# Retention's score-times-value products written ahead of every read of their PSUM bank, with the keys' transpose in the other bank, and the rotation tables fetched from GpSimd's queue

## The chip, the cores and the metric

The kernel runs on one core of a Trainium2 chip. The metric is the device time of one execution in microseconds (us); the time of a kernel is the median of its runs. A core has five engines with instruction streams of their own: TensorE (PE in the profile; its weight loads are shown as PEld), VectorE (DVE), ScalarE (ACT), GpSimd (POOL) and SyncE (SP), which here only issues transfers. Each engine takes its instructions in a fixed order, and an instruction whose operands aren't ready holds up what is written behind it on that engine. TensorE writes its results into PSUM, which is divided into eight banks of 512 float32 per partition; VectorE and ScalarE read them from there. Transfers between DRAM and SBUF are issued from a queue of SyncE, ScalarE or GpSimd.

## The reference

One decoder layer over 2048 positions of width 1024, causal, batch 1, in float32. A normalised and modulated input `h` goes through one projection of 9216 columns, whose parts feed two sequence mixers: HGRN2 (a gated linear recurrence, 8 heads, states of 128 x 128) and multi-scale retention (8 heads, keys of 64, values of 128). Both are normalised by head, gated, mixed and projected out. The change touches retention, which the reference computes in chunks of 128 positions:

```python
scores = einsum('bhnid,bhnjd->bhnij', qc, kc) * Dm[:, None]
intra = einsum('bhnij,bhnje->bhnie', scores, vc)
chunk_state = einsum('bhnjd,bhnde->...', kc * zeta, vc)     # summed over the chunk's positions j
R_next = chunk_decay * R + chunk_state
cross = einsum('bhnid,bhnde->bhnie', qc * xi, R)
o = intra + cross
```

`q` and `k` are rotated first, which needs tables of cosines and sines by position:

```python
rotary(t) = concatenate([t1 * cos - t2 * sin, t1 * sin + t2 * cos])
```

## The kernel before

**Projection.** The 2048 positions are worked in two halves of 1024 (`sb` 0 and 1), each in two blocks of 512. The projection's columns are cut into groups of 256, called quads; `ORDER` lists them: `a` (HGRN2's forget gate and query of a head), `v` (a value group of both mixers), `b` (retention's q and k of a pair of heads), `A` and `B` (the gates). Each quad is computed by a Strassen-like scheme of seven products instead of eight. A product has 12 matmuls of 128 x 512 (float32 split in a high and a low part, three matmuls for each of four k-tiles). TensorE's instructions are kept in program order by the class `InOrder` (L70 for matmuls, L73 for transposes), so the order in which the Python code writes them is the order of execution. For the other engines a planner orders the instructions, by priorities and by a model of costs: the splitting of weights (`Weights.split`, tiles `b` from `w`; ScalarE at L295, VectorE at L296 and L416) has 400 steps of priority, the evacuation of products (`after`, tiles `c`, `x`, `vt`) 600. Three buffers hold split weights (`NBW`), four hold temporaries (tag `tp`, `NTP`), and PSUM's eight banks are shared out as `x0`, `x1`, `v` (products), `lv` (HGRN2's tree), two of tag `o` and one tile `rt` of two banks.

**Background.** The mixers run between the products as generators, called lanes. `Background.tick` counts one for each k-tile of a product, and when eight have gone by (`GAP`) a `burst` takes each lane one step on: retention's lane first, then HGRN2's `tree` and `hgrn_out`. A lane that yields `"mid"` is taken on once more in the same burst, after the others have had their turn.

**Retention.** `retention(p, sb)` handles a pair of heads over eight chunks, in nine steps; four pairs and two halves make eight passes. In step n it begins chunk n and ends chunk m = n − 1. It has one PSUM tile of two banks, `pt` (named `rt` in the profile), and one bank of tag `o`, `po` (named `por`). The step's work is written in this order: the transpose of chunk n's keys (`kz`, in `pt`'s second bank); its scores for both heads (one in each bank of `pt`); for chunk m the part that comes from the state (`cross`, one head in `po`, the other in `pt`'s second bank); the update of the state (`x`, in `pt`'s first bank). VectorE then reads the scores and multiplies them by the decay (`scm`, L985), ScalarE reads the keys (`rkz`, L988), and VectorE reads `x` into the state `rs` (L991, or L995 in the first chunk). After `yield "mid"`, and so behind what the other lanes put on TensorE, the score-times-value products of chunk m are written: they add `scms[m]` times the values onto `pos[0]` in `po` and onto `pos[1]` in `pt`'s second bank. `normed` then takes the squares (ScalarE, L827), the reciprocal root (GpSimd, L174 or L176, and L177) and the scaled copies (ScalarE, L830) into `ur`. HGRN2's `normed` goes the same way, with `ssh`, `rrh` and `uh`. `pt` has one buffer, so step n + 1 writes it when step n has been read.

**Rotation.** `tables` writes cosines and sines (and their negative) to a DRAM tensor `lin`. For each `b` quad `load_rot` fetches, for each of two blocks, a cosine tile `ct` with one transfer (L626) and a sine tile `sn` with two (L628), broadcast over the heads, into temporaries of tag `tp`. `take_b` multiplies on VectorE (L639 to L642) and stores the rotated tiles to DRAM, from where retention reads them. The load for the first block is written ahead of the quad's first product, the one for the second block ahead of the next quad's. All transfers but the weights' are issued from SyncE's queue; the weights are issued from ScalarE's.

The functions that the change touches, and what calls them:

Of the kernel before, what the change touches and what calls it, by code (L numbers as in the profile page):

```python
# [22 lines left out]
P = 128  # L23
# [5 lines left out]
BLK = 512  # L29
# [33 lines left out]
def tile_hybrid(ctx: ExitStack, tc: tile.TileContext, a: dict, out: bass.AP):  # L63
    nc = tc.nc
    V, S, G = nc.vector, nc.scalar, nc.gpsimd
# [9 lines left out]
    PE = InOrder()  # L75
# [10 lines left out]
    def bank(name, tag):  # L86
        return pp.tile([P, 512], F32, name=name, tag=tag, bufs=small[tag])

    def tmp(name, cols=512):
        return upool.tile([P, cols], F32, name=name, tag="tp", bufs=NTP)  # L90

    def dram(name, shape):
        return dpool.tile(shape, F32, name=name, tag=name)
# [41 lines left out]
    for t in range(8):  # L135
        tag, bufs = xwhere[t]
        n = {"f": 2 * 513, "k": 1025, "q": 1024, "A": 1024}[tag]
# [465 lines left out]
    lin = dram("lin", [3, 32, L])  # L603
# [18 lines left out]
    def load_rot(q, tb):  # L622
        b = QUADS[q][0] * NBLK + tb
        ct, sn = tmp(f"ct{q}_{tb}"), tmp(f"sn{q}_{tb}")
        sl = slice(b * BLK, (b + 1) * BLK)
        nc.sync.dma_start(out=ct, in_=lin[0, :, sl].unsqueeze(0).broadcast_to([4, 32, BLK]))  # L626
        for two in range(2):
            nc.sync.dma_start(  # L628
                out=sn[64 * two : 64 * two + 64, :], in_=lin[1 + two, :, sl].unsqueeze(0).broadcast_to([2, 32, BLK])
            )  # L630
        rots[tb] = ct, sn
# [190 lines left out]
    def normed(pos, dsts, nm, eps=None):  # L822
        n = len(pos)
        ss = upool.tile([P, 2], F32, name=f"ss{nm}", tag="ss", bufs=4)
        rr = upool.tile([P, 2], F32, name=f"rr{nm}", tag="rr", bufs=4)
        for i in range(n):
            S.activation(out=junk, in_=pos[i], func=AF.Square, accum_out=ss[:, i : i + 1])  # L827
        rstd_of(rr[:, 0:n], ss[:, 0:n], P, eps)
        for i in range(n):
            S.activation(out=dsts[i], in_=pos[i], func=AF.Copy, scale=rr[:, i : i + 1])  # L830

    def send_u(s, h, b, c, u):

        def store():
            nc.sync.dma_start(out=ud[s, h, b][:, (c - 1) * P : (c + 1) * P], in_=u.rearrange("p c e -> p (c e)"))
            if c == 3:
                usent[s, h, b] = bg.now

        bg.post(5.0, store)
# [82 lines left out]
    def retention(p, sb):  # L922
        h0 = 2 * p
        g0 = sb * CH
        while rnext[0] != (sb, p):
            yield True
        rs = upool.tile([P, P], F32, name=f"rs{p}_{sb}", tag="rs", bufs=1)
        if sb:
            nc.sync.dma_start(out=rs, in_=rstd_d[p])
        qks, kzs, vrs, scms, age, u = {}, {}, {}, {}, {}, {}  # L930
        rows = [slice(64 * j, 64 * j + 64) for j in range(2)]
        dT = upool.tile([P, 256], F32, name=f"dT{p}_{sb}", tag="dT", bufs=1)
        nc.sync.dma_start(out=dT, in_=a["dT"][:, h0 * P : (h0 + 2) * P])

        def fetch(n):
            g = g0 + n
            qks[n] = upool.tile([P, 2, P], F32, name=f"rqk{p}_{g}", tag="rqk", bufs=NQP)
            sl = slice(n * P, (n + 1) * P)
            nc.sync.dma_start(out=qks[n], in_=rd[p, sb][:, :, sl].rearrange("s p t -> p s t"))
            age[n] = bg.now  # L940

        def fetch_v(n):
            g = g0 + n
            vrs[n] = upool.tile([P, 2, P], F32, name=f"vr{p}_{g}", tag="vr", bufs=2)
            sl = slice(n * P, (n + 1) * P)
            nc.sync.dma_start(out=vrs[n], in_=vdr[p, sb][:, sl, :].rearrange("j t e -> t j e"))

        n = nf = 0
        while n <= CH:
            while nf < CH and nf <= n + 1:  # L950
                b = sb * NBLK + nf // 4
                ts = [rsent.get((s, p, b)) for s in range(2)] + [vsent.get((1, h0 + j, b)) for j in range(2)]
                if any(t is None or t > bg.now - 5.0 for t in ts):
                    break
                fetch(nf)
                nf += 1
            if n < CH and (n not in age or bg.now < age[n] + 6.0):
                yield True
                continue
            if n < CH:  # L960
                fetch_v(n)
            m, g = n - 1, g0 + n - 1
            last = g == L // P - 1
            pt = pp.tile([P, 2, 512], F32, name=f"rt{p}_{g0 + n}", tag="rt", bufs=1)
            x = pt[:, 0, P : 2 * P]
            if n < CH:
                kz = pt[:, 1, 2 * P : 3 * P]
                PE.transpose(out=kz, in_=qks[n][:, 1, :], identity=ident)
                for j, r in enumerate(rows):
                    PE.matmul(out=pt[:, j, 0:P], lhsT=qks[n][r, 1, :], rhs=qks[n][r, 0, :], start=True, stop=True)  # L970
            if n:
                vb_ = [vrs[m][:, j, :] for j in range(2)]
                po = bank(f"por{p}_{g}", "o")
                pos = [po[:, 0:P], pt[:, 1, P : 2 * P]]
                if g:
                    for j, r in enumerate(rows):
                        PE.matmul(
                            out=pos[j], lhsT=qks[m][r, 0, :], rhs=rs[r, :], start=True, stop=False, skip_group_check=True
                        )
                if not last:  # L980
                    for j, r in enumerate(rows):
                        PE.matmul(out=x[r, :], lhsT=kzs[m][:, r], rhs=vb_[j], start=True, stop=True)
            if n < CH:
                scms[n] = upool.tile([P, 2, P], F32, name=f"scm{p}_{g0 + n}", tag="scm", bufs=2)
                V.tensor_tensor(out=scms[n], in0=pt[:, :, 0:P], in1=dT.rearrange("p (j t) -> p j t", j=2), op=ALU.mult)  # L985
                kzs[n] = upool.tile([P, P], F32, name=f"rkz{p}_{g0 + n}", tag="rkz", bufs=2)
                for j, r in enumerate(rows):
                    S.activation(out=kzs[n][:, r], in_=kz[:, r], func=AF.Copy, scale=zeta[:, h0 + j : h0 + j + 1])  # L988
            if n:
                if g and not last:  # L990
                    V.scalar_tensor_tensor(  # L991
                        out=rs, in0=rs, scalar=gC[:, p : p + 1], in1=x, op0=ALU.mult, op1=ALU.add
                    )
                elif g == 0:
                    V.tensor_copy(out=rs, in_=x)  # L995
                yield "mid"
                for j in range(2):
                    PE.matmul(
                        out=pos[j], lhsT=scms[m][:, j], rhs=vb_[j], start=g == 0, stop=True, skip_group_check=True
                    )  # L1000
                b = g // 4
                if m % 2 == 0:
                    for j in range(2):
                        u[j] = upool.tile([P, 2, P], F32, name=f"ur{h0 + j}_{g}", tag="ur", bufs=4)
                normed(pos, [u[j][:, m % 2, :] for j in range(2)], f"r{p}_{g}", epsx[:, h0 : h0 + 2])
                if m % 2:
                    for j in range(2):
                        send_u(1, h0 + j, b, m % 4, u[j])
                if m == CH - 1:
                    rnext[0] = (sb, p + 1) if p + 1 < NP else (sb + 1, 0)  # L1010
                    if not last:
                        nc.sync.dma_start(out=rstd_d[p], in_=rs)
            n += 1
            yield
# [297 lines left out]
    mid = max(i for i, q in enumerate(QUADS) if q[0] == 0)  # L1312
    for i in range(2, len(seq)):
        m, q = seq[i]
# [7 lines left out]
        if kind == "b" and m == 2:  # L1322
            load_rot(q, 0)
        if m == 2 and QUADS[q - 1][1] == "b":
            load_rot(q - 1, 1)
# [8 lines left out]
        if q == NQ - 1:  # L1334
# [4 lines left out]
            if m == 4:  # L1339
# [3 lines left out]
                    out=pro["fg"], in0=pro["fg"], scalar1=float(D) ** 0.5, scalar2=None, op0=ALU.mult  # L1343
# [116 lines left out]
```

## Time and profile before

| | |
|---|---|
| median of three runs | 2314.5 us (2307.4 to 2316.7) |
| the profiled execution | 2308.1 us, span 2306.3 us |
| TensorE busy | 2007.8 us, 87% |
| VectorE busy | 1426.5 us, 62% |
| ScalarE busy | 1006.0 us, 44% |
| GpSimd busy | 239.6 us, 10% |
| mean granted TensorE clock | 0.951 of full speed |
| transfers | 263 MB; SyncE's queue 27.8%, ScalarE's 11.6% of the 16 DMA engines' time |

A group row of the page names a line, an engine, an operation, the tiles it writes and reads, their shapes and the count; then the busy time, the mean of one instruction in ns, the idle time of the engine just before these instructions, and what ended most of that idle time. `rt<-vr,scm` are the score-times-value products into the tile `rt`, `b<-w` is the splitting of weights. A row of waits reads "engine, tile and line, waited for engine, tile and line: us in total, times, longest". In an answer in order of time, the brackets hold the idle time ahead of the instruction and what ended it. What ends a wait is inferred from semaphores. Idle time of an engine costs something only where the end depends on it.

### The profile page before, as it was taken

What the parts mean: (1) busy time and instruction counts of PE and PEld (TensorE: products, weight loads), DVE (VectorE), ACT (ScalarE), POOL (GpSimd) and SP (SyncE); (2) the same over time, 40 slices, a digit from 0 to 9 for tenths busy, and PEclk for the clock granted to TensorE, in tenths of its full rate; (3) what the DMA queues carried; (4) which work ended last, traced back from release to release, by engine and by line L of the source; (5) the groups of instructions that cost most, each with busy time, mean ns of one, the idle gap of its engine ahead of it and who ended that gap; (6) DMA issues with size and microseconds to landing.
All of it is one profiled execution on the core that took longest, in us unless ns stands there. A gap on an engine that the chain in (4) does not pass through costs nothing.

```text
span 2306.3 us, 39796 instructions
## 1 busy us (share of the span) xinstructions
PE 2007.8 (87%) x15108; PEld 1612.8 (70%) x15108; DVE 1426.5 (62%) x2677; ACT 1006.0 (44%) x2434; POOL 239.6 (10%) x466
## 2 busy tenths in 40 slices
PE   4878799997989698889778899997999799898998
PEld 3656588776767576668666688776777677676887
DVE  5865667565756466656765667565767575658333
ACT  5624344534455354444524444543454345444232
POOL 1001110201020110210000110101011000110000
PEclk9989999999999799989989999999999899999999
DMA  8143424242344437624434424242244424235443
GB/s 272 42 101 103 109 76 105 81 115 85 85 132 128 135 117 207 194 76 125 151 82 104 112 78 107 83 111 86 75 133 130 119 65 108 74 93 170 134 137 119
DMA packets 446016, 263.02 MB, mean 114 GB/s; under 512 B 161024, under 2 KB 395520, under 8 KB 445824
## 3 DMA queue, kind: packets, MB, share of 16 engines
q1 hardware_dynamic: 292704, 184.43, 27.8%
q10 hardware_dynamic: 153120, 76.04, 11.6%
q8 instruction: 119, 1.95, 0.4%
q14 instruction: 73, 0.60, 0.1%
HBM read 188.03 MB, written 72.35 MB: 113 GB/s over the span
## 4 chain that ended last, share of the span: by engine, by line
PE 53%; DMA 15%; DVE 14%; ACT 8%; issue 4%; POOL 4%; SPq 1%; ACTq 1%; DVEq 0%; POOLq 0%
PE x L70 22%; PE v L70 11%; PE ops L70 8%; PE y L70 5%; DVE b L296 4%; ACT b L295 2%; DVE w L416 2%; DMA w<-in_w_a_dram 2%; PE lv L70 2%; PE poh L70 2%; DMA w<-in_w_d_dram 2%; DMA rd<-c 2%; POOL rrh L177 1%; DMA sn<-lin 1%; PE rt L70 1%
## 5 line engine op out<-in xcount | busy, mean ns | idle before, releaser
L296 DVE TENSOR_TENSOR b<-w,b 128x512 fp32r<-128x512 f32 (+1 forms) x553 | 346.2, 635 | 329.0 <-ACT b L295 321.4
L295 ACT ACTIVATE b<-w 128x512 fp32r<-128x512 f32 (+1 forms) x553 | 316.7, 583 | 388.0 <-PE x L70 297.0
L70 PE MATMUL v<-S,b 128*128 128x512 f32 x1704 | 433.7, 404 | 26.5 <-ACT c L477 19.7
L70 PE MATMUL x<-S,b 128*128 128x512 f32 x1704 | 431.9, 402 | 4.8 <-DVE b L296 3.2
L70 PE MATMUL x<-A,b 128*128 128x512 f32 x1704 | 430.1, 401 | 2.3 <-ACT c L477 0.9
L70 PEld LDWEIGHTS v<-S,b 128*128 128x128 f32 x1704 | 323.7, 193 | 99.9 <-ACT c L477 22.4
L70 PEld LDWEIGHTS x<-A,b 128*128 128x128 f32 x1704 | 323.1, 193 | 70.9 <-ACT wo L295 1.3
L70 PEld LDWEIGHTS x<-S,b 128*128 128x128 f32 x1704 | 320.9, 193 | 72.5 <-DVE b L296 4.5
L70 PE MATMUL y<-A,b 128*128 128x512 f32 x840 | 221.9, 416 | 47.2 <-DVE vt L588 39.5
L416 DVE TENSOR_TENSOR w<-w,w 128x512 f32<-128x512 f32 x284 | 194.9, 687 | 66.6 <-DMA w<-in_w_a_dram 21.7
L70 PEld LDWEIGHTS y<-A,b 128*128 128x128 f32 x840 | 165.6, 201 | 84.5 <-issue 49.4
L174 POOL TENSOR_SCALAR ssh<-ssh 128x1 f32<-128x1 f32 x128 | 44.6, 349 | 1447.9 <-ACT junk L827 1447.8
L70 PE MATMUL ops<-wo,m 128*128 128x512 f32 x768 | 176.5, 392 | 0.0
L70 PEld LDWEIGHTS ops<-wo,m 128*128 128x128 f32 x768 | 145.7, 190 | 30.5
L477 ACT ACTIVATE c<-v 128x512 f32<-128x512 f32 x142 | 84.5, 595 | 119.8 <-PE v L70 109.1
L70 PE MATMUL rt<-vr,scm 128*128 128x128 f32 x128 | 32.7, 340 | 90.5 <-DVE rs L991 80.3
L830 ACT ACTIVATE uh<-poh,rrh 128x128 f32<-128x128 f32 x128 | 47.1, 368 | 142.1 <-POOL rrh L177 142.0
L497 DVE TENSOR_TENSOR c<-c,x 128x512 f32<-128x512 f32 x71 | 48.8, 687 | 88.9 <-PE x L70 88.3
L70 PEld LDWEIGHTS lv<-q,k 128*32 128x32 f32 (+1 forms) x5888 | 70.8, 110 | 45.7 <-issue 35.8
L70 PE MATMUL lv<-q,k 128*32 128x16 f32 (+2 forms) x5888 | 82.1, 188 | 19.9 <-DVE ad L788 8.2
L177 POOL TENSOR_TENSOR rrh<-ssh,mhalf 128x1 f32<-128x1 f32 x128 | 93.1, 727 | 10.6
L70 PEld LDWEIGHTS rt<-vr,scm 128*128 128x128 f32 x128 | 20.6, 202 | 101.1 <-DVE rs L991 89.7
(189 smaller groups left out, 2463.0 us busy)
## 6 DMA issues: line engine op xcount, KB each, us to landing
w<-in_w_d_dram ACTq DMA_DIRECT2D x128, 256.0 KB
w<-in_w_c_dram ACTq DMA_DIRECT2D x66, 256.0 KB
mu<-ud SPq DMA_DIRECT2D x64, 256.0 KB
w<-in_w_a_dram ACTq DMA_DIRECT2D x60, 256.0 KB
wa<-in_w_ada_dram SPq DMA_DIRECT2D x16, 512.0 KB
w<-in_w_b_dram ACTq DMA_DIRECT2D x32, 256.0 KB
vd<-vt SPq DMA_DIRECT2D x128, 64.0 KB
vh<-vd SPq DMA_DIRECT2D x64, 128.0 KB
```

The source lines that it names most:

```text
L70: return tc.keep_in_program_order(nc.tensor.matmul(**kw))
L174: G.tensor_scalar(out=ss, in0=ss, scalar1=n * EPS, scalar2=None, op0=ALU.add)
L177: G.tensor_tensor(out=dst, in0=ss, in1=mhalf.broadcast_to([P, w]), op=ALU.pow)
L295: S.activation(out=t[0], in_=src, func=AF.Copy)
L296: return V.tensor_tensor(out=t[1], in0=src, in1=t[0], op=ALU.subtract)
L416: V.tensor_tensor(out=out, in0=x, in1=y, op=ALU.add)
L477: S.activation(out=t, in_=ps, func=AF.Copy)
L497: V.tensor_tensor(out=t, in0=t, in1=xb[q], op=ALU.subtract)
L830: S.activation(out=dsts[i], in_=pos[i], func=AF.Copy, scale=rr[:, i : i + 1])
```

## The change

Two edits. In `load_rot` the three transfers of a load are issued from GpSimd's queue (`G`) instead of SyncE's. In `retention` the bank `po` is taken at the start of each step, the first one too, and holds the keys' transpose `kz` as well as `pos[0]`; the score-times-value products are written right behind the state update's matmuls, ahead of the three reads by VectorE and ScalarE; the `yield "mid"` is gone, so that `normed` too is written ahead of the other lanes' work in the burst. What is computed stays the same.

```diff
@@ load_rot
-        nc.sync.dma_start(out=ct, in_=lin[0, :, sl].unsqueeze(0).broadcast_to([4, 32, BLK]))
+        G.dma_start(out=ct, in_=lin[0, :, sl].unsqueeze(0).broadcast_to([4, 32, BLK]))
         for two in range(2):
-            nc.sync.dma_start(
+            G.dma_start(
                 out=sn[64 * two : 64 * two + 64, :], in_=lin[1 + two, :, sl].unsqueeze(0).broadcast_to([2, 32, BLK])
             )
@@ retention
             x = pt[:, 0, P : 2 * P]
+            po = bank(f"por{p}_{g0 + n}", "o")
             if n < CH:
-                kz = pt[:, 1, 2 * P : 3 * P]
+                kz = po[:, P : 2 * P]
                 PE.transpose(out=kz, in_=qks[n][:, 1, :], identity=ident)
                 for j, r in enumerate(rows):
                     PE.matmul(out=pt[:, j, 0:P], lhsT=qks[n][r, 1, :], rhs=qks[n][r, 0, :], start=True, stop=True)
             if n:
                 vb_ = [vrs[m][:, j, :] for j in range(2)]
-                po = bank(f"por{p}_{g}", "o")
                 pos = [po[:, 0:P], pt[:, 1, P : 2 * P]]
...
                 if not last:
                     for j, r in enumerate(rows):
                         PE.matmul(out=x[r, :], lhsT=kzs[m][:, r], rhs=vb_[j], start=True, stop=True)
+                for j in range(2):
+                    PE.matmul(
+                        out=pos[j], lhsT=scms[m][:, j], rhs=vb_[j], start=g == 0, stop=True, skip_group_check=True
+                    )
             if n < CH:
                 scms[n] = upool.tile([P, 2, P], F32, name=f"scm{p}_{g0 + n}", tag="scm", bufs=2)
...
                 elif g == 0:
                     V.tensor_copy(out=rs, in_=x)
-                yield "mid"
-                for j in range(2):
-                    PE.matmul(
-                        out=pos[j], lhsT=scms[m][:, j], rhs=vb_[j], start=g == 0, stop=True, skip_group_check=True
-                    )
                 b = g // 4
```

## The prediction, made before the changed kernel was run

> **What bounds the kernel now.** I read four views: the page, TensorE's waits by releaser, the eight retention passes side by side, and single steps in order of time. The page first.
>
> ```profile
> span 2306.3 us, 39796 instructions
> PE 2007.8 (87%) x15108; PEld 1612.8 (70%) x15108; DVE 1426.5 (62%) x2677; ACT 1006.0 (44%) x2434; POOL 239.6 (10%) x466
> ...
> L295 ACT ACTIVATE b<-w 128x512 fp32r<-128x512 f32 (+1 forms) x553 | 316.7, 583 | 388.0 <-PE x L70 297.0
> ...
> L70 PE MATMUL rt<-vr,scm 128*128 128x128 f32 x128 | 32.7, 340 | 90.5 <-DVE rs L991 80.3
> ```
>
> TensorE is busy 87%, and the weight splitting that feeds it (`b<-w`) spends 297.0 us waiting for TensorE to give back a buffer: on the whole TensorE sets the pace, its instructions run in written order, and a wait at its head is lost unless a later wait would have come anyway. Of its idle 298.5 us (2306.3 − 2007.8) the last row holds 90.5 in one group: retention's score-times-value products into `rt`. They number 128; the waits (total, times, longest):
>
> ```profile
> PE rt L70 <- DVE rs L991: 80.3, 48, 8.1
> ...
> PE rt L70 <- DVE rs L995: 10.1, 4, 5.6
> ...
> PE rt L70 <- ACT ur L830: 4.0, 2, 2.0
> ...
> PE x L70 <- DVE b L296: 3.2, 1, 3.2
> ```
>
> So 52 of the 64 retention steps stop TensorE for 1.74 us on average (90.5 / 52), while waits for split weights are small. One step in order of time (start, length, engine; in brackets the idle time before it and what ended it):
>
> ```profile
> 228.66 0.49 PE L70 MATMUL rt<-rqk 64*128 64x128 f32 x4
> ...
> 232.50 0.42 DVE L985 TENSOR_TENSOR scm<-rt,dT 128x256 f32<-128x256 f32 x1
> ...
> 232.96 0.52 ACT L988 ACTIVATE rkz<-rt,zeta 128x64 f32<-128x64 f32 x2 [3.18 <-DVE scm L985]
> ...
> 233.69 0.34 DVE L991 SCALAR_TENSOR_TENSOR rs<-rs,gC,rt 128x128 f32<-128x128 f32 x1
> ...
> 234.09 0.49 PE L70 MATMUL rt<-vr,scm 128*128 128x128 f32 x2 [2.33 <-DVE rs L991]
> ...
> 236.29 0.27 ACT L827 ACTIVATE junk<-rt 128x128 bf16<-128x128 f32 x1
> ...
> 237.00 0.70 POOL L177 TENSOR_TENSOR rrr<-ssr,mhalf 128x2 f32<-128x2 f32 x1
> ...
> 238.00 0.36 ACT L830 ACTIVATE ur<-rt,rrr 128x128 f32<-128x128 f32 x1
> ...
> 239.87 0.27 PE L73 MATMUL rt<-ident,rqk 128*128 128x128 f32 x1
> ```
>
> The scores stand at 229.2, but VectorE, busy with rotation and weights, reads them only at 232.50; ScalarE's key copies wait for that read, the state update for the copies, and the product, which needs none of the three results (its `scm` is the previous step's), for the state update. It is an ordering of accesses to one PSUM tile, not data.
>
> **Part 1: products ahead of the reads, keys in the other bank.** No instruction is added or removed beyond one more allocation of an "o" bank per pass (eight). Removed is the cause of the 90.5 us: all matmuls of a step, the two products included, now precede the reads of `rt`, and their operands are a step old. What follows the product on TensorE is the next projection product, 12 matmuls. How much stays won depends on what is late next.
>
> ```profile
> 193.00:290.00 97.00, 72.30 (x731) 56.49 (x730) 56.32 (x116) 39.15 (x127) 13.28 (x28) 0.93 0.38 105
> ...
> sum 683.00, PE 574.09 PEld 452.58 DVE 406.53 ACT 324.94 POOL 124.44; mean PE 71.76 PEld 56.57 DVE 50.82 ACT 40.62 POOL 15.55
> ```
>
> These are the eight retention passes (length; busy PE, weight loads, DVE, ACT, POOL; granted clock; DMA): 683 us, VectorE busy 406.5. With 90.5 us taken out VectorE would be busy 69% (406.5 / 592.5), up from 60%. It does not become the bound, but its local backlog grows, since it used TensorE's stalls to catch up. So I split the 90.5. Five waits are long:
>
> ```profile
> 210.98 0.79 PE L70 MATMUL rt<-vr,scm 128*128 128x128 f32 x2 [5.60 <-DVE rs L995]
> 270.88 0.80 PE L70 MATMUL rt<-vr,scm 128*128 128x128 f32 x2 [8.07 <-DVE rs L991]
> 943.40 0.80 PE L70 MATMUL rt<-vr,scm 128*128 128x128 f32 x2 [4.94 <-DVE rs L991]
> 1254.71 0.80 PE L70 MATMUL rt<-vr,scm 128*128 128x128 f32 x2 [5.65 <-DVE rs L991]
> 1279.93 0.79 PE L70 MATMUL rt<-vr,scm 128*128 128x128 f32 x2 [4.59 <-DVE rs L991]
> ```
>
> They sum to 28.9 us, and there VectorE itself was held or overfull; before 270.88 it stood on a weight transfer:
>
> ```profile
> 269.27 0.69 DVE L416 TENSOR_TENSOR w<-w,w 128x512 f32<-128x512 f32 x1 [5.69 <-DMA w<-in_w_a_dram]
> ...
> 271.32 4.26 PE L70 MATMUL y<-A,b 128*128 128x512 f32 x12
> 275.42 2.88 PE L70 MATMUL x<-S,b 128*128 128x512 f32 x12
> ```
>
> TensorE will run into the products already prepared (three split buffers, 2.88 us each at full rate) and then wait for the same late weights. Bounds 0 and 28.9; I take 10, two of the five as wholly won, nearer the low end because the transfer ends no sooner. The other 47 waits hold 90.5 − 28.9 = 61.6 us, 1.3 us each. Their cover is the three prepared buffers; bounds 30 (half comes back as waits for VectorE's backlog) and 61.6; I take 49, 80%, nearer the top because weight splitting is what waits for TensorE (297.0 us), not the reverse.
>
> **What the moved steps now wait for.** The key transpose writes a fresh "o" bank, and the scores write `rt`; both need the previous step's last ScalarE read, `ur`. In the step shown it ends at 238.36 and the next transpose starts at 239.87. Without the stall that start moves to 237.54; the read comes sooner too, because its squares need no matmul after the state update: that update ends at 234.03, and from square to last copy the chain above lasts 2.1 us (236.29 to 238.36 in the trace, two squares, two GpSimd instructions, two copies), so about 236.4 with the queue ahead of it. Slack stays near 1.1 us; steps with less wait. Today that wait costs 4.0 us; I let it grow by 3. On ScalarE the key copies no longer stand for VectorE; instead the squares of `rt` stand for the state update, so I count nothing there (if squares are late, the wait just named is what grows).
>
> **Part 2: tables from GpSimd's queue.** Sixteen loads, three transfers each, leave SyncE's queue for GpSimd's.
>
> ```profile
> L628 SPq DMA_DIRECT2D sn<-lin x32: 475/512/540, 120.7 to 1818.9; - x32
> ...
>   DMA sn<-lin: 32.3, 12
> ...
>   DVE sw L639: 17.4, 6
>   DVE sw L640: 14.8, 6
> ```
>
> ```profile
> L626 SPq DMA_DIRECT2D ct<-lin x16: 578/584/3318, 119.9 to 1817.5; - x16
> ```
>
> ```profile
> L174 POOL TENSOR_SCALAR ssh<-ssh x128: 218/222/1055, 185.2 to 2059.7; 128x1 f32<-128x1 f32 x128
> L177 POOL TENSOR_TENSOR rrh<-ssh,mhalf x128: 547/573/1695, 185.5 to 2060.3; 128x1 f32<-128x1 f32 x128
> ...
>   ACT uh L830: 142.0, 127
> ```
>
> SyncE spends 0.58 + 2 × 0.51 = 1.6 us issuing a load. No GpSimd issue is in this trace. Bounds: 0.51 us each (SyncE's) and 1.70 (GpSimd's longest instruction), so 1.5 to 5.1 us a load; I take 1 us each, 3 us a load, as GpSimd's ordinary instructions (0.2 to 0.6) are nearer the low end. Behind a load on GpSimd stand the norm's two instructions, on which ScalarE already waits 142.0 us. GpSimd is busy 10%, so most loads fall into gaps; at this one the next norm follows within 2.5 us:
>
> ```profile
> 1232.49 0.58 SPq L626 DMA_DIRECT2D ct<-lin  x1
> 1233.18 1.04 SPq L628 DMA_DIRECT2D sn<-lin  x2
> ...
> 1234.95 0.22 POOL L174 TENSOR_SCALAR ssh<-ssh 128x1 f32<-128x1 f32 x1 [3.89 <-ACT junk L827]
> ```
>
> I count four such meetings at 1 us, 4 us lost (bounds 0; 16 × 5.1 = 82 if every load met one). VectorE waits 32.3 us for tables already (each of the two multiplies six times: six of the eight loads for a second half block), so a later landing hits it directly, and a sooner one helps: from a queue of its own a load no longer stands behind SyncE's stores and loads. Bounds +32.3 (all gone) and −28 (eight loads × 3.5 us, 5.1 against 1.6); I take +2, the middle. SyncE's freed 26 us are worth nothing: no wait for its queue is among TensorE's.
>
> [...]
>
> **Sum.** 49 + 10 − 3 − 4 + 2 = 54 us. The profiled execution took 2308.1 us beside its span of 2306.3; 2308.1 − 54 = 2254. That execution lies near the lowest of the three runs (2307.4, 2314.5, 2316.7), about 4 us under their middle, so I say 2258 for a median. Its own range, with the 61.6 kept between 50% and 100% and the long waits between 0 and 20: 2230 to 2290.
>
> **Rivals.**
> 1. *The stall moves on.* Without its pauses VectorE falls behind and TensorE waits for split weights and evacuations instead; only a third of 61.6 is kept, none of the long ones: 20 us, about 2293. For it: VectorE's backlog caused every one of these waits. Against: the splitting waits for TensorE, and 69% is no bound.
> 2. *Slower: GpSimd's queue as the bottleneck.* A load's issue waits on GpSimd for its free temporary, as it does on SyncE now, and whatever is behind it waits too:
>
> ```profile
> 1270.30 0.58 SPq L626 DMA_DIRECT2D ct<-lin  x1
> ...
> 1275.49 1.07 SPq L628 DMA_DIRECT2D sn<-lin  x2
> ```
>
> Here 4.6 us pass between cosine and sine. With 3.5 us of slower issue and 4.6 of such waiting each load lands d = 8.1 us later, VectorE stands eight times that, 65 us, and four norms are held 4 us each, 16: 2312 − 56 + 81 = 2337. It decides from d = 5, where 40 + 16 cancel the 56 of part 1. For it: GpSimd's order is as fixed as TensorE's. Against: GpSimd idles 90%, and in the passes it is busy 124.4 of 683. [...]
> 3. *More than forecast.* All 61.6 and most of the long waits stay won, and tables land sooner and free half of the 32.3: 61.6 + 20 + 16 = 98, about 2215.
> 4. *Nothing moves.* The tile's accesses stay serialized elsewhere (the scores then wait for `ur`): about 2312.
>
> **Chances.** Forecast 0.54; stall moves on 0.17; slower 0.12; more 0.10; nothing 0.07. Three runs of this kernel scatter by 0.4%, so under 0.5% (12 us) counts as no change. Faster: 0.54 + 0.15 + 0.10 = 0.79; within: 0.02 of rival 1 and 0.07, 0.09; slower 0.12. The range 2208 to 2318 leaves out the slower case and the far end of "more".
>
> **What would show it.** Right: the idle time before `rt<-vr,scm` falls from 90.5 to under 5 us, key copies no longer wait for `scm` (3.18 in the step shown), TensorE's idle total falls by 50 to 60, and no other releaser in its waits grows by over 15. Wrong: waits for `b`, `c` or `ur` grow by 40 or more (rival 1); the waits of `sw` for `sn` go above 60 us and those of `uh` for `rrh` above 180 (rival 2); below 16 us of `sn` waits is rival 3. The forecast fails if the product still waits for a read, or if planning anew moves the VectorE order enough to bring stalls at other places.

## The result, and the profile after

The changed kernel takes 2225.6 us (2222.3 to 2232.8 over four runs) against 2311.0 us for the kernel before, measured beside it: a ratio of 0.9633, 95% interval 0.9598 to 0.9668, so 85 us or 3.7% less. It is faster, as forecast, and inside the range on record, but the gain is larger than the 54 us of the sum, and the time lies 4 us below the forecast's own range of 2230 to 2290.

The profiled execution took 2225.1 us. From its page, the span and the busy times; then the group of the score-times-value products, from TensorE's groups by shape (busy time, mean ns, idle time before them):

```profile
span 2223.3 us, 40029 instructions
PE 1998.1 (90%) x15108; PEld 1611.3 (72%) x15108; DVE 1421.4 (64%) x2677; ACT 1002.2 (45%) x2434; POOL 275.5 (12%) x514
```

```profile
L70 PE MATMUL rt<-vr,scm 128*128 128x128 f32 x128 | 26.0, 286 | 0.0
```

The 90.5 us before this group are gone to the last tenth. TensorE's idle total fell from 298.5 to 225.2 us (2223.3 − 1998.1), by 73, and its busy time by 10. TensorE's waits after, as far as the prediction spoke of them (total, times, longest):

```profile
PE y L70 <- DVE vt L588: 32.3, 4, 10.1
...
PE uT L73 <- ACT c L477: 22.6, 16, 3.0
...
PE rt L70 <- ACT ur L830: 9.9, 5, 3.1
...
PE por L73 <- ACT ur L830: 2.9, 2, 2.1
```

The wait for the previous step's norm (`ur`) grew from 4.0 to 12.8 us, that of the gates' transposes for evacuation from 15.2 to 22.6; no other wait grew by more than about 6 us. One step in order of time:

```profile
1418.32 0.49 PE L70 MATMUL rt<-rqk 64*128 64x128 f32 x4
...
1419.66 0.39 PE L70 MATMUL rt<-vr,scm 128*128 128x128 f32 x2
...
1420.78 0.42 DVE L989 TENSOR_TENSOR scm<-rt,dT 128x256 f32<-128x256 f32 x1
1420.95 0.52 ACT L992 ACTIVATE rkz<-por,zeta 128x64 f32<-128x64 f32 x2 [0.89 <-PE poh L70]
1421.12 0.34 DVE L995 SCALAR_TENSOR_TENSOR rs<-rs,gC,rt 128x128 f32<-128x128 f32 x1
...
1424.20 0.36 ACT L830 ACTIVATE ur<-rt,rrr 128x128 f32<-128x128 f32 x1
...
1427.05 0.27 PE L73 MATMUL por<-ident,rqk 128*128 128x128 f32 x1
```

The product follows the scores by 1.3 us without a wait, ScalarE's key copies run beside VectorE's decay product instead of behind it, and the norm's last copy ends 2.5 us before the next transpose (1424.56 to 1427.05). The tables, from the view of the tile `sn` (issue in ns, waits for it, time from issue to landing):

```profile
L628 POOL DMA_DIRECT2D sn<-lin x32: 651/658/720, 119.8 to 1747.4; - x32
...
  DMA sn<-lin: 13.7, 4
...
DMA to landing us min/median/max: 5.6/7.0/10.7
```

VectorE's waits for the sines fell from 32.3 to 13.7 us. GpSimd takes 0.66 us for the issue of a sine, and the spread is small.

### The profile page after: what moved, and what is told of

It reads as the page before. It is cut to its first block, busy times and chain, and to the rows that moved or that the text cites. A ratio compares the mean times of both kernels' runs of the same rounds, so it can differ in the third digit from the quotient of the medians.

```text
span 2223.3 us, 40029 instructions
## 1 busy us (share of the span) xinstructions
PE 1998.1 (90%) x15108; PEld 1611.3 (72%) x15108; DVE 1421.4 (64%) x2677; ACT 1002.2 (45%) x2434; POOL 275.5 (12%) x514
## 4 chain that ended last, share of the span: by engine, by line
PE 40%; DVE 9%; DMA 9%; ACT 4%; issue 3%; POOL 2%; SPq 1%; ACTq 0%; DVEq 0%; POOLq 0%
PE x L70 15%; PE ops L70 8%; PE v L70 8%; PE y L70 4%; DVE b L296 2%; PE poh L70 1%; ACT b L295 1%; DMA w<-in_w_b_dram 1%; PE lv L70 1%; DMA sn<-lin 1%; DMA w<-in_w_d_dram 1%; DVE w L416 1%; PE uT L73 1%; PE rt L70 1%; POOL rrh L177 1%
## 5 line engine op out<-in xcount | busy, mean ns | idle before, releaser
L70 PE MATMUL y<-A,b 128*128 128x512 f32 x840 | 218.4, 411 | 40.1 <-DVE vt L588 32.3
L776 DVE TENSOR_TENSOR q<-q,f 128x512 f32<-128x512 f32 x112 | 76.8, 685 | 19.6 <-PE lv L70 19.5
L477 ACT ACTIVATE c<-y 128x512 f32<-128x512 f32 x70 | 41.7, 596 | 98.4 <-PE y L70 98.4
L177 POOL TENSOR_TENSOR rrh<-ssh,mhalf 128x1 f32<-128x1 f32 x128 | 82.8, 647 | 10.5
```

The lines of the kernel that those rows point to most:

```text
L70: return tc.keep_in_program_order(nc.tensor.matmul(**kw))
L177: G.tensor_tensor(out=dst, in0=ss, in1=mhalf.broadcast_to([P, w]), op=ALU.pow)
L477: S.activation(out=t, in_=ps, func=AF.Copy)
L776: V.tensor_tensor(out=qv, in0=qv, in1=tv[:, :, :, 0:1].broadcast_to([P, NU, nb, m]), op=ALU.mult)
```

## The experiments

Each run was timed beside the kernel before, on one chip for each group of runs; the ratios are to that. Gains and differences are worked out from these ratios, times the 2311 to 2318 us of the kernel before.

### The two edits apart

Retention's edit alone, which is the changed kernel with the tables back on SyncE's queue:

```diff
-        G.dma_start(out=ct, ...)          # and the two sine transfers
+        nc.sync.dma_start(out=ct, ...)
```

> The changed kernel with the three table transfers back on SyncE's queue: retention's edit alone. Theory A (the retention edit carries nearly all of the gain of 85 us, and the tables' queue is worth under 10): 2225 to 2240 us, idle time before the score-times-value products 0 to 5 us, VectorE's waits for the sine tables about 30 us as before. Theory B (my sum for retention, 56 us, was right, and the tables bring the other 30): about 2255 us with the same idle time.

2265.8 us, ratio 0.9781 (0.9757 to 0.9806): 51 us of gain. The table edit alone, on the kernel before:

```diff
-        nc.sync.dma_start(out=ct, ...)    # and the two sine transfers
+        G.dma_start(out=ct, ...)
```

> The kernel before with the table transfers on GpSimd's queue, nothing else. Theory A: 2303 to 2316 us, no difference that can be told. Theory B: about 2281 us. Theory C (the queue costs time, because the norms stand behind the transfers on GpSimd): 2320 or more, with ScalarE's waits for the reciprocal root above 150 us in place of 142.

2281.3 us, ratio 0.9845 (0.9819 to 0.9872): 36 us of gain. The two ratios multiplied give 0.963, the changed kernel's. So the gains add up, theory A fell, and theory B holds: the tables are at the 2281 us that it said, retention is 11 us slower. My forecast for retention's part (56 us) was near its measured size; the missing gain was all in the part that I had put at −2.

### Inside retention's edit: order, bank, and the place of the norm

Products ahead of the reads, keys left in the two-bank tile, tables on SyncE's queue:

```diff
-                kz = po[:, P : 2 * P]
+                kz = pt[:, 1, 2 * P : 3 * P]
```

> Retention's products ahead of the reads, but the keys' transpose stays in the second bank of the two-bank tile; tables on SyncE's queue. If the order of TensorE's work is the whole cause: within 5 us of the run with the whole retention edit, and the waits of ScalarE's key copies for VectorE's decay product stay near 50 us without a price. If ScalarE, held at the key copies, delays evacuation and splitting: 15 to 30 us slower than that run, about 2250 to 2260.

2278.6 us, ratio 0.9846 (0.9812 to 0.9880): 36 us of gain, 15 less than the whole edit. ScalarE's waits, and then TensorE's, in this kernel:

```profile
ACT rkz L992 <- DVE scm L989: 48.2, 31, 6.1
```

```profile
PE uT L73 <- ACT c L477: 29.8, 17, 3.5
...
PE rt L73 <- ACT ur L830: 13.8, 6, 8.5
...
PE rt L70 <- ACT ur L830: 5.0, 3, 1.7
```

So the 48 us for which ScalarE stands at the key copies aren't free, as the second of the two expectations had it: TensorE waits longer for ScalarE, 18.8 us for the norm (`ur`, two rows) where the whole retention edit has 12.6, and 29.8 us at the gates' transposes (`uT` for `c`) where it has 21.1. The keys alone, on the kernel before:

```diff
-                kz = pt[:, 1, 2 * P : 3 * P]
+                kz = po[:, P : 2 * P]
```

(with `po` taken at the start of the step)

> The kernel before with the keys' transpose moved to the other bank, products still behind the reads and behind the other lanes; tables on SyncE's queue. If the stall is the product standing behind VectorE's reads of the two-bank tile: idle time before the products stays at 75 to 90 us and the time at 2295 to 2312 us, a little sooner because the state update no longer waits for ScalarE's key copies (6.8 us in the kernel before). If the key copies were what held the chain: idle time under 50 us and about 2275.

2296.0 us, ratio 0.9909 (0.9879 to 0.9938): 21 us of gain. TensorE's waits:

```profile
PE rt L70 <- DVE rs L991: 39.5, 38, 8.4
...
PE por L70 <- ACT rkz L988: 13.1, 14, 3.1
```

The idle time before the products into `rt` halves (39.5 and 3.1 for the first chunks, from 90.5): about half of the stall hung on the key copies, against my expectation of 75 to 90 us, and the time is in the range that went with it because a part comes back elsewhere: 13.1 us as a new wait, since the other product now shares its bank with the keys, and 7.8 us at the gates' transposes (`uT` for `c`, from 15.2 to 23.0).

The hand-over put back, between the products and the norm, in the changed kernel:

```diff
+                yield "mid"
                 b = g // 4
```

> The changed kernel with the hand-over to the other lanes put back, now between the products and the norm: TensorE's order is the changed kernel's, only the norm's instructions are written behind the other lanes' again. If the position of the norm is worth nothing: 2220 to 2230 us. If the earlier norm frees the two-bank tile and the o bank sooner, as in my slack of 1.1 us: 2235 to 2255, with TensorE's waits for the norm's copies above the 12.8 us (9.9 and 2.9) of the changed kernel.

2258.9 us, ratio 0.9769 (0.9741 to 0.9797): 32 us more than the changed kernel, and only about 18 us less than the table edit alone (0.9845), though the products are ahead of the reads here too. TensorE's waits:

```profile
PE rt L70 <- ACT ur L830: 27.8, 21, 4.0
```

That is 4 us above what I gave the case of a norm that matters. With the norm behind the other lanes' work, `ur` comes late and the next step's writes of `rt` wait 21 times; `uT` for `c` grows too, from 22.6 to 33.0 us. The idle time before the products is 0.0 here as well. So the stall can be gone whole and the edit be worth no more than what the keys' bank brought alone (21 us, there with the tables on SyncE's queue): the order with a late norm adds nothing that shows. And the hand-over taken from the kernel before, so that the norm is early but the products stay behind the reads:

```diff
-                yield "mid"
```

> The kernel before without the hand-over: products still behind the reads, but the products and the norm ahead of the other lanes' work. TensorE then stands at the products with nothing of the other lanes before them: the idle time before them grows from 90.5 to 130 to 200 us. If that decides: 2330 to 2380 us. If the earlier norm, which was worth 33 us where the products were ahead, makes up for it: 2295 to 2325.

2398.2 us, ratio 1.0362 (1.0329 to 1.0395): 84 us slower, and 18 us beyond the upper of my two ranges. TensorE's group of the products, and the span with the granted clock of this kernel; the kernel before has 0.951:

```profile
L70 PE MATMUL rt<-vr,scm 128*128 128x128 f32 x128 | 34.9, 360 | 125.7 <-DVE rs L991 113.1 <-DVE rs L995 12.6
```

```profile
core: us from the first to the last instruction, mean granted TensorE clock
core 0: 2393.7 us, clock 0.930
```

The other lanes' matmuls had covered 35 us of the wait (90.5 against 125.7). The larger part of the loss is TensorE's busy time, which is 48 us longer (last section). The order of the products is what allows the norm to go early; the early norm is what makes the order pay.

### Inside the table edit: queue or spread

What the queue edit takes away is in VectorE's waits. With retention's edit alone the rotation's multiplies wait 20.1 us for the first sine and 15.7 for the second (rows below); in the changed kernel 13.7 and nothing, and the 7.6 us in which they stood for stores of `vt`, whose buffers they reuse, are gone. Together this is 30 us, and TensorE's idle time is 31 us shorter (256.3 to 225.2). The waits for weights did not fall: 69.6 us with retention's edit alone, 76.6 in the changed kernel:

```profile
DVE w L416 <- DMA w<-in_w_b_dram: 26.8, 6, 6.8
...
DVE w L416 <- DMA w<-in_w_a_dram: 22.4, 6, 5.8
...
DVE w L416 <- DMA w<-in_w_d_dram: 21.4, 6, 6.5
...
DVE w L416 <- DMA w<-in_w_c_dram: 6.0, 3, 3.7
```

Two views of the kernel before show how a load goes from SyncE's queue: the transfer engines' share (tenths, half a microsecond a column) and rate from 1815 to 1835 us, then VectorE's two multiplies that wait for the sines:

```profile
DMA  2716139422223211039991111111111111117994
GB/s 70 250 30 194 51 110 292 139 94 106 102 109 104 64 20 33 16 113 348 325 251 36 48 50 47 50 47 51 45 49 49 53 49 53 49 53 223 304 393 185
```

```profile
1826.90 0.69 DVE L639 TENSOR_TENSOR sw<-c,sn 64x512 f32<-64x512 f32 x1 [5.93 <-DMA sn<-lin]
...
1830.14 0.69 DVE L640 TENSOR_TENSOR sw<-c,sn 64x512 f32<-64x512 f32 x1 [2.56 <-DMA sn<-lin]
```

For some 7 us the engines are at one tenth, at 45 to 53 GB/s, and the second sine lands about 3 us after the first, though their issues are half a microsecond apart, as if one went after the other through a small part of the engines. The load isn't alone there: two stores of rotated tiles were issued from 1820.99 to 1822.76, and the share stays at one tenth until 1833, after both sines have landed. Tables from SyncE's queue, in pieces of 32 rows without a broadcast dimension:

```diff
+        for j in range(4):
+            nc.sync.dma_start(out=ct[32 * j : 32 * j + 32, :], in_=lin[0, :, sl])
+        for j in range(4):
+            nc.sync.dma_start(out=sn[32 * j : 32 * j + 32, :], in_=lin[1 + j // 2, :, sl])
```

> The changed kernel, but the tables come from SyncE's queue again, each load as eight transfers of 32 rows instead of three broadcast ones. In the kernel before a load keeps the transfer engines at one tenth to an eighth of their capacity (47 to 53 GB/s for some 7 us), as if it ran on two of the sixteen. Theory A (the gain of the table edit is the spread of the load over all engines; a transfer of 32 rows is spread on SyncE's queue too): 2220 to 2235 us, near the changed kernel's 2225, VectorE's waits for the sines at 15 us or less. Theory B (it is the queue: GpSimd's is free while SyncE's has other waits and transfers ahead): 2260 to 2270 us, as the retention edit alone (2266), VectorE's waits for the sines near 30 us.

2210.9 us, ratio 0.9546 (0.9518 to 0.9575): faster than the changed kernel by some 20 us and than retention's edit alone by 54, and 9 us under theory A's lower end. VectorE's waits with retention's edit alone, and then with the pieces:

```profile
DVE w L416 <- DMA w<-in_w_a_dram: 24.7, 6, 6.0
...
DVE sw L639 <- DMA sn<-lin: 20.1, 6, 6.0
...
DVE w L416 <- DMA w<-in_w_d_dram: 19.7, 6, 5.2
...
DVE w L416 <- DMA w<-in_w_b_dram: 17.4, 3, 6.3
...
DVE sw L640 <- DMA sn<-lin: 15.7, 6, 2.9
```

```profile
DVE w L416 <- DMA w<-in_w_a_dram: 27.8, 6, 7.4
...
DVE w L416 <- DMA w<-in_w_c_dram: 5.1, 3, 2.7
...
DVE w L416 <- DMA w<-in_w_d_dram: 2.3, 5, 0.8
```

The waits for the sines are gone, and those for weights fell by half, from 69.6 to 35.2 us: the weights, issued from ScalarE's queue, had been held up by the tables. So a load doesn't need GpSimd's queue to land in time; in its old form it gains from that queue, in pieces it is in time from SyncE's. As finely cut, but by columns, with the broadcast dimension kept:

```diff
+        for i in range(2):                                       # hc, hl: the columns of half i
...
+            nc.sync.dma_start(out=ct[:, hc], in_=lin[0, :, hl].unsqueeze(0).broadcast_to([4, 32, 256]))
+            for two in range(2):
+                nc.sync.dma_start(
+                    out=sn[64 * two : 64 * two + 64, hc],
+                    in_=lin[1 + two, :, hl].unsqueeze(0).broadcast_to([2, 32, 256]),
+                )
```

> The changed kernel with the tables from SyncE's queue in six broadcast transfers, each of half the columns: as finely cut as the run with 32-row transfers, but with the four- and two-row outer dimension of the kernel before. Theory A (what counts is over how many engines a transfer is spread, and the outer dimension sets it): 2255 to 2275 us, near the retention edit alone (2266), and VectorE's waits for the sines at 25 us or more. Theory B (several smaller transfers are what helps, by being in flight together): 2210 to 2235.

2253.2 us, ratio 0.9738 (0.9712 to 0.9764): 2 us under what theory A allowed, 10 us below retention's edit alone and 44 us above the pieces by rows, with the waits for the sines back:

```profile
DVE sw L643 <- DMA sn<-lin: 29.0, 5, 8.5
...
DVE sw L644 <- DMA sn<-lin: 3.3, 3, 1.3
```

So 44 of the 54 us hang on the form of the transfer and not on how many there are. Cutting a load by rows takes away both the outer dimension and the broadcast, and no run parts these two; the stores of the next section have the outer dimension without a broadcast. The pieces by rows from GpSimd's queue:

```diff
-        G.dma_start(out=ct, in_=lin[0, :, sl].unsqueeze(0).broadcast_to([4, 32, BLK]))
+        for j in range(4):
+            G.dma_start(out=ct[32 * j : 32 * j + 32, :], in_=lin[0, :, sl])    # the sines likewise
```

> The changed kernel with eight transfers of 32 rows for each load, on GpSimd's queue: five more issues of 0.66 to 0.79 us, some 3.5 us more of GpSimd's time for each of sixteen loads. It measures how much GpSimd's time weighs. Theory A (GpSimd has room, the load's end moves by 3.5 us and eight loads are near the time of need): 2230 to 2250 us. Theory B (its issue time is hidden altogether): 2222 to 2229. Theory C (the norms behind it hold ScalarE and the whole step): over 2260.

2215.2 us, ratio 0.9574 (0.9550 to 0.9597), better than any of the three theories allowed, and by the intervals not to be told from the pieces on SyncE's queue. Five more issues cost nothing that shows: an issue takes 0.50 us here, and a piece, which has half the bytes of a broadcast sine (64 against 128 KB), lands in half the time (median 3.5 against 7.0 us):

```profile
L629 POOL DMA_DIRECT2D sn<-lin x64: 496/496/498, 120.7 to 1723.9; - x64
...
DMA to landing us min/median/max: 2.0/3.5/7.9
```

### The same cause elsewhere

The stores of the rotated queries and keys have an outer dimension of two as well. In the changed kernel:

```diff
-                nc.sync.dma_start(out=dst[two], in_=r[64 * two : 64 * two + 64, :])
+                for h in range(2):
+                    r0 = 64 * two + 32 * h
+                    nc.sync.dma_start(out=dst[two][h], in_=r[r0 : r0 + 32, :])
```

> The changed kernel with the stores of the rotated queries and keys in four transfers of 32 rows instead of two of 64, which have the same two-row outer dimension as the sine loads. Theory A (they, too, run on two engines, and hold up what shares these): faster than the changed kernel by 5 to 25 us, 2200 to 2220. Theory B (nobody waits for these stores, or the two extra issues cost what is won): 2220 to 2232.

2185.0 us, ratio 0.9442 (0.9419 to 0.9466): 44 us faster than the changed kernel, well beyond theory A. SyncE's own waits for these stores, ahead of reading the tiles back, fell from 34.0 to 15.1 us, and VectorE's waits for weights sum to 35 us, against 77 in the changed kernel:

```profile
DVE w L416 <- DMA w<-in_w_b_dram: 26.2, 6, 6.7
...
DVE w L416 <- DMA w<-in_w_c_dram: 5.1, 3, 2.7
...
DVE w L416 <- DMA w<-in_w_d_dram: 3.8, 4, 2.0
...
DVE w L416 <- DMA w<-in_w_a_dram: 0.3, 1, 0.3
```

Both in pieces, all on SyncE's queue:

```diff
+        nc.sync.dma_start(...)     # tables as in the first run with pieces, stores as just above
```

> The retention edit with tables (eight transfers) and stores of the rotated queries and keys (four) all in 32-row transfers on SyncE's queue. If the gains of the two add up (55 us for the tables over the retention edit alone, 41 for the stores over the changed kernel): about 2170 us. If both only relieve the same stretches, and what is left is VectorE's and TensorE's own: 2180 to 2190, as with the stores alone (2185).

2185.3 us, ratio 0.9437 (0.9405 to 0.9470): the same as the stores alone. The waits for weights and sines are down to 12 us together, and yet nothing more is won: what remains ahead of TensorE is VectorE's and ScalarE's own work (`y` for `vt` 35.4 us, `uT` for `sz` 22.8, `y` for `ro` 19.1). The last of these was 7.7 us in the kernel before and 1.6 in the changed one; why it grows was not tried. Either of the two versions beats both the kernel before and the changed one.

## Why the prediction was right, and where it was wrong

**What bounds the kernel: right.** The stall of 90.5 us was an order of accesses, it went wholly, and VectorE (64% busy) did not become the bound. Rival 1 as a whole fell: no wait of TensorE in the changed kernel grew by more than 9 us. Part of it is true all the same. With retention's edit alone TensorE's idle total fell by 42 us (298.5 to 256.3), so that 48 of the 90.5 came back in other places, the products' wait for ScalarE's evacuation first of all (`v` for `c`, from 19.7 to 30.0 us). Rival 4 fell with the 0.0 before the products.

**Part 1: the size right, in part by luck.** 49 + 10 − 3 = 56 us were forecast, 51 measured (45 to 56 by the interval). The sum earns them all by ending the stall. With the stall ended and the norm behind the other lanes the edit is worth about 18 us, and the early norm brings 32 more. The prediction saw that the norm's read comes sooner, but used this only to keep a slack of 1.1 us (it is 2.5 in the step shown); the wait that it named there, for `ur`, grew by 9 us and not by 3. "I count nothing there", of ScalarE's key copies that no longer stand for VectorE (50.8 us), was wrong as well: the keys' bank is worth 15 us on top of the order. How much of the 28.9 us of long waits was kept, no run separates.

**Part 2: the term that failed.** +2 − 4 = −2 us was forecast, and 36 measured alone, 34 on top of retention's edit. Three steps of the working failed. "From a queue of its own a load no longer stands behind SyncE's stores and loads" is not what had held the loads: in 32-row pieces the same rows, issued from SyncE's own queue, aren't waited for at all (2211 us). The bound of +32.3 counted only VectorE's waits for the sines. With the table edit alone these fell by half, from 32.3 to 15.7 us; what the bound lacked are effects of the move on other transfers, such as the same multiplies' waits for stores of `vt`, 8.8 us before and none after. And "the middle" between far bounds was a choice without a row, where the transfer engines' share in a load's stretch would have been one: one tenth for 7 us is in the trace of before. The issue price (1 us taken, 0.66 to 0.79 measured) was near enough, and the meetings with norms, 4 us in the sum, don't show: with the table edit alone ScalarE's wait for `rrh` is 141.3 us, against 142.0. Rival 2 has nothing for it. The sines' issues on GpSimd last 0.65 to 0.72 us, without a stretched one among 32.

**Of the tests named beforehand**, the idle time, the key copies and "no other releaser" came out as forecast; TensorE's idle total fell by 73 instead of 50 to 60; and the waits for the sines, 13.7 us, met the mark of rival 3, whose "tables land sooner" is what happened. Its time, 2215, was 10 us too low, and its split was off too: 82 us from retention and 16 from the tables, where 51 and 34 were measured.

**What stays open.** That these loads use a small part of the engines is read from share and rate (one tenth, 45 to 53 GB/s, in a stretch that two stores share); which engines, no trace here shows, and why GpSimd's queue helps loads in the old form no run takes by itself. What the runs show is the form: in 32-row pieces from SyncE's queue the sines aren't waited for, while in pieces by columns most of the wait stays (29.0 and 3.3 us, against 20.1 and 15.7 with retention's edit alone). The wait for the second sine, these 15.7 us, is gone in the changed kernel. That the form and the queue act through the spread over the engines is my reading of this; no run shows it.

## What to carry to other kernels

Where an in-order engine stands at an instruction whose operands are long ready, look for reads of the same PSUM tile ahead of it, and move the write before the reads together with what follows from it, here the norm (the idle time before the products went from 90.5 to 0.0 us); either move alone was worth little (the order with a late norm, nothing that shows beyond the keys' bank) or did harm (the early norm alone, 84 us). When a load is late, look at the share and rate of the transfer engines in that stretch before blaming its queue: here, stretches with transfers of an outer dimension of two ran at one tenth of the engines (45 to 53 GB/s in the one shown), and cutting the transfers by rows is a change of a few lines, worth 54 us for the tables over retention's edit alone and 44 for the stores over the changed kernel. A bound on what a faster transfer brings must include the waits for the other transfers beside it, as those for weights here, which fell by half, from 69.6 to 35.2 us, when the loads were cut by rows.

## What the runs showed of the hardware that was not expected

In the run without the hand-over TensorE's stalls went with a loss beyond their length. Its idle time rose by 40 us (298.5 to 338.1) and its busy time by 48 for the same matmuls (2007.8 to 2055.6), with a granted clock of 0.930 in place of 0.951; busy time times clock is the same, 1909 and 1912 us. The four runs of that kernel have clocks of 0.927 to 0.936, those of the kernel before 0.942 to 0.952. In the fastest runs busy time is 1982 to 1987 us at 0.957 and 0.958. More idle time doesn't always go with a lower clock, though: retention's edit alone has 42 us less of it than the kernel before, and its clock is 0.943. In the kernel before one long stall is seen in windows of 10 us (length, busy PE, weight loads, DVE, ACT, POOL, granted clock, DMA):

```profile
890.00:900.00 10.00, 10.00 (x51) 8.41 (x50) 3.33 (x6) 6.26 (x13) 0.79 (x2) 1.00 0.84 228
900.00:910.00 10.00, 3.12 (x17) 2.52 (x15) 6.27 (x10) 2.24 (x6) 0.79 (x2) 0.78 0.71 226
910.00:920.00 10.00, 7.93 (x30) 6.17 (x30) 3.39 (x5) 2.21 (x4) 0.00 (x0) 0.71 0.78 235
```

TensorE is busy for 3.1 us of the second window, and the clock stays low into the third, when it works again. That the clock and not something else makes the busy time longer is argued from these numbers; no run changed it by itself, and what sets it is not shown.
